# Gate and up products of a SwiGLU in seven half-size products instead of eight, with the weight differences formed by accumulating DMAs

## The chip, the cores and the metric

The kernel runs on one core of one Trainium2 chip. The metric is the device time of one execution in microseconds, lower is better. TensorE (PE) multiplies, with PEld the loading of its stationary operand; VectorE (DVE), ScalarE (ACT) and GpSimd (POOL) do the elementwise work; SyncE (SP) issues the plain DMAs.

## The reference

One layer of a transformer trunk in float32, for 512 tokens (plus 16 meta tokens in the attention) of width 1024:

```python
for i in range(DEPTH):            # DEPTH = 1
    mix = dsa_attention(h, w_in, w_o, rel_bias, k_top)
    h = layer_norm(ALPHA * h + mix, ln1_g, ln1_b)
    ffn = (jax.nn.silu(h @ w_gate) * (h @ w_up)) @ w_down   # 1024 -> 2816 -> 1024
    h = layer_norm(ALPHA * h + ffn, ln2_g, ln2_b)
return h[:, N_META:]
```

The change is in the two products `h @ w_gate` and `h @ w_up`, and in what prepares their operands and takes up their results.

## The kernel before

A float32 product is made of three products of a rounded type (float32r): each operand x is parted into hi (x rounded, a copy by ACT) and lo (x - hi, a subtraction, line 159), and hi\*hi, hi\*lo and lo\*hi are added up in PSUM (lines 286 to 288 for gate and up, line 1072 for the down product).

The order of the instructions on each engine is the order in which the Python code issues them (`manual_schedule`); a tile pool gives each tile a buffer, and a wait is put in where a buffer or a value is not yet free.

The stages of the program are the projections and the sparse attention (to about 300 us), the second half of the output projection with the first normalisation (to 313 us), gate and up (313 to 555 us), down (555 to 677 us) and the last normalisation.

Gate and up: the 2816 columns of each weight make 22 blocks f of 128 columns. For each block the chunks `wg{f}` and `wu{f}` (128 partitions x 8 K-tiles x 128 columns, 512 KB each) are loaded by SP two chunks ahead, parted one chunk ahead (`cut`, called by `ahead`; hi by ACT, lo of gate by DVE and lo of up by POOL), and multiplied with the 512 normalised tokens `h1h`, `h1l`, which lie turned (K on the partitions): 8 K-tiles x 3 terms x 2 weights make 48 matmuls of 128x512. Block 0 runs in two halves of 256 tokens, because the norms of the last two token blocks of 128 come late: `turn_norm` (line 971) turns token block b by TensorE and parts it. After each block ACT takes the silu of gate (line 1013), DVE multiplies it with up (line 1014), and the result is parted at once into `hh`, `hl`, which are the stationary operands of the down product.

Down: for each half `th` of the tokens, all 22 chunks of `wd` are loaded, parted and multiplied (line 1072).

Of the kernel before, what the change touches and what calls it, by code (L numbers as in the profile page):

```python
# [117 lines left out]
def trunk(ctx, tc, a, out):  # L118
# [848 lines left out]
    def turn_norm(b):  # L967
        for q in range(2):
            pt = bank(f"tz{b}{q}", "pt")
            for i in range(4):  # L970
# [4 lines left out]
            sub(nc.vector, lo, ptv, hi)

    for b in range(NB):
# [8 lines left out]
        if b == 0:  # L986
            load(g_ff, 2)


    hh, hl = [], []  # L990
    hq = []

    def widen(nm, o, n0, n1):
        wh, wl = chunk(nm)
        return mm3(
            o[:, n0:n1],
            ((wh[:, k * P : (k + 1) * P], wl[:, k * P : (k + 1) * P], h1h[k][:, n0:n1], h1l[k][:, n0:n1]) for k in range(KT)),
        )

    for f in range(NF):  # L1000
        pg = [bank(f"p_wg{f}", "mm"), bank(f"p_wu{f}", "S")]

        for n0, n1 in ((0, 2 * P), (2 * P, S)) if f == 0 else ((0, S),):
            for o, nm in zip(pg, (f"wg{f}", f"wu{f}")):
                if n1 == S:
                    ahead(nm)
                for k, _ in enumerate(widen(nm, o, n0, n1)):
                    if n1 < S and k == LATER_K:
                        turn_norm(2 + (nm == "wu0"))
        if f == NF - 1:  # L1010
            ahead("wd0_0")
        sg = third(f"sg{f}")[:, :S]
        nc.scalar.activation(sg, pg[0], AF.Silu)
        nc.vector.tensor_tensor(out=sg, in0=pg[1], in1=sg, op=ALU.mult)  # L1014
        if f < 8:
            if f % 4 == 0:
                hq.append((quad(f"hh{f}", S), quad(f"hl{f}", S)))
            hi, lo = (x[:, f % 4] for x in hq[f // 4])
        else:
            hi, lo = unit(f"hh{f}", F32R)[:, :S], unit(f"hl{f}", F32R)[:, :S]  # L1020
        act_copy(hi, sg)
        sub(nc.vector, lo, sg, hi)
        hh.append(hi)
        hl.append(lo)
# [129 lines left out]
```

## Time and profile before

| what | value |
|---|---|
| time, median of 3 runs | 685.97 us (685.8 to 687.2) |
| the profiled execution: its own time | 686.96 us |
| its span in the trace | 685.2 us |
| granted TensorE clock, mean | 0.996 of 2.4 GHz |
| PE busy | 669.6 us (98%) |
| DVE, ACT, POOL busy | 418.9, 287.3, 237.8 us |
| gate and up, blocks 1 to 21 | 326.7 to 555.2 us |

The page gives the busy time of each engine over the whole span. The views by line, by window and in order of time cut it into stages; the span and the time of the execution differ by 1.8 us that lie outside the trace.

### The profile page before, as it was taken

What the parts mean: (1) busy time and instruction counts of PE and PEld (TensorE: products, weight loads), DVE (VectorE), ACT (ScalarE), POOL (GpSimd) and SP (SyncE); (2) the same over time, 40 slices, a digit from 0 to 9 for tenths busy, and PEclk for the clock granted to TensorE, in tenths of its full rate; (3) what the DMA queues carried; (4) which work ended last, traced back from release to release, by engine and by line L of the source; (5) the groups of instructions that cost most, each with busy time, mean ns of one, the idle gap of its engine ahead of it and who ended that gap; (6) DMA issues with size and microseconds to landing.
All of it is one profiled execution on the core that took longest, in us unless ns stands there. A gap on an engine that the chain in (4) does not pass through costs nothing.

```text
span 685.2 us, 9428 instructions
## 1 busy us (share of the span) xinstructions
PE 669.6 (98%) x3440; PEld 565.6 (83%) x3440; DVE 418.9 (61%) x797; ACT 287.3 (42%) x516; POOL 237.8 (35%) x240
## 2 busy tenths in 40 slices
PE   8999999999999999999999999999999999999995
PEld 6888787889998888889888888888888888888884
DVE  5589897888888887696334243343433355575426
ACT  5473512567777775614323233232322334423310
POOL 2063812497786676653212121221212200011003
PEclk9999999999999999999999999999999999999998
DMA  6547130543133346410131322313132267745611
GB/s 235 173 148 258 58 75 17 152 152 85 56 103 87 93 114 211 154 62 31 63 122 63 123 80 105 114 70 123 61 123 83 102 224 233 244 152 193 195 51 61
DMA packets 31807, 83.11 MB, mean 121 GB/s; under 512 B 3745, under 2 KB 8913, under 8 KB 31761
## 3 DMA queue, kind: packets, MB, share of 16 engines
q1 hardware_dynamic: 31328, 82.12, 36.9%
q8 instruction: 27, 0.44, 0.3%
q10 hardware_dynamic: 432, 0.39, 0.2%
...
HBM read 74.86 MB, written 5.27 MB: 117 GB/s over the span
## 4 chain that ended last, share of the span: by engine, by line
PE 51%; DVE 1%; POOL 0%; DVEq 0%; issue 0%
PE pd L1072 17%; PE p_wu L288 6%; PE p_wu L287 6%; PE p_wu L286 6%; PE p_wg L288 6%; PE p_wg L287 6%; PE p_wg L286 6%; DVE su L1082 0%; POOL fr L939 0%; DVE y L1081 0%; DVE y L956 0%; PE tz L971 0%; DVE mw L1087 0%; DVEq L1150 0%; DVE y L958 0%
## 5 line engine op out<-in xcount | busy, mean ns | idle before, releaser
L159 POOL TENSOR_TENSOR l_wu<-r_wu,h_wu 128x1024 fp32r<-128x1024 f32 x22 | 52.8, 2401 | 179.5 <-ACT h_wu L156 179.5
L1014 DVE TENSOR_TENSOR sg<-p_wu,sg 128x512 f32<-128x512 f32 x22 | 15.2, 692 | 107.8 <-PE p_wu L288 107.8
L159 DVE TENSOR_TENSOR l_wd<-r_wd,h_wd 128x1024 fp32r<-128x1024 f32 x36 | 45.4, 1263 | 41.9 <-ACT h_wd L156 41.7
L286 PE MATMUL p_wg<-h1h,h_wg 128*128 128x512 f32 (+1 forms) x184 | 70.0, 380 | 0.0
L286 PE MATMUL p_wu<-h1h,h_wu 128*128 128x512 f32 (+1 forms) x184 | 70.0, 380 | 0.0
L287 PE MATMUL p_wg<-h1l,h_wg 128*128 128x512 f32 (+1 forms) x184 | 69.9, 380 | 0.0
L288 PE MATMUL p_wu<-h1h,l_wu 128*128 128x512 f32 (+1 forms) x184 | 69.9, 380 | 0.0
L287 PE MATMUL p_wu<-h1l,h_wu 128*128 128x512 f32 (+1 forms) x184 | 69.9, 380 | 0.0
L288 PE MATMUL p_wg<-h1h,l_wg 128*128 128x512 f32 (+1 forms) x184 | 69.9, 380 | 0.0
L159 DVE TENSOR_TENSOR l_wg<-r_wg,h_wg 128x1024 fp32r<-128x1024 f32 x21 | 52.8, 2513 | 24.4 <-ACT h_wg L156 24.4
L156 ACT ACTIVATE hh<-sg 128x512 fp32r<-128x512 f32 x22 | 13.9, 632 | 119.3 <-DVE sg L1014 119.3
L670 POOL TENSOR_TENSOR lg<-lg,rec 128x144 f32<-128x144 f32 (+1 forms) x64 | 52.6, 846 | 21.9 <-DVE rec L668 21.1
L1072 PE MATMUL pd<-h_wd,hh 128*128 128x512 f32 (+1 forms) x162 | 59.6, 368 | 0.0
L1072 PE MATMUL pd<-h_wd,hl 128*128 128x512 f32 (+1 forms) x162 | 59.6, 368 | 0.0
L1072 PE MATMUL pd<-l_wd,hh 128*128 128x512 f32 (+1 forms) x162 | 59.5, 368 | 0.0
L156 ACT ACTIVATE h_wd<-r_wd 128x1024 fp32r<-128x1024 f32 x36 | 38.0, 1060 | 46.5 <-DMA r_wd<-in_wd 22.2
L644 POOL TENSOR_TENSOR bm<-score,tz 128x256 f32<-128x256 f32 (+1 forms) x64 | 43.9, 716 | 16.4 <-DVE mn L653 14.9
L939 POOL TENSOR_TENSOR fr<-fr,half_neg 128x1 f32<-128x1 f32 x4 | 4.0, 1004 | 117.5 <-DVE fr L938 117.0
L661 ACT ACTIVATE lg<-lg,mn 128x272 f32<-128x272 f32 (+1 forms) x64 | 36.3, 571 | 11.6 <-DVE mn L653 11.6
L287 PEld LDWEIGHTS p_wu<-h1l,h_wu 128*128 128x128 f32 x184 | 34.6, 188 | 6.6
L286 PEld LDWEIGHTS p_wg<-h1h,h_wg 128*128 128x128 f32 x184 | 34.6, 188 | 6.5
L286 PE MATMUL p_k<-hTh,h_wk 128*128 128x264 f32 x128 | 37.7, 295 | 2.3 <-DVE q L329 2.3
...
## 6 DMA issues: line engine op xcount, KB each, us to landing
r_wd<-in_wd SPq DMA_DIRECT2D x36, 512.0 KB, 4.3
r_wg<-in_wg SPq DMA_DIRECT2D x22, 512.0 KB, 3.7
r_wu<-in_wu SPq DMA_DIRECT2D x22, 512.0 KB, 4.5
...
r_wq<-in_wq SPq DMA_DIRECT2D x8, 512.0 KB, 4.8
r_wk<-in_wk SPq DMA_DIRECT2D x8, 512.0 KB, 3.4
rbig<-rdram SPq DMA_DIRECT2D x1, 3072.0 KB, 15.0
...
```

The lines of the kernel that those rows point to most:

```text
L156: nc.scalar.activation(o, i, AF.Copy, scale=scale)
L159: eng.tensor_tensor(out=o, in0=x, in1=y.bitcast(F32), op=ALU.subtract)
L286: nc.tensor.matmul(o, lh, rh, start=i == 0, stop=False)
L287: nc.tensor.matmul(o, lh, rl, start=False, stop=False)
L288: nc.tensor.matmul(o, ll, rh, start=False, stop=i == KT - 1)
L644: nc.gpsimd.tensor_tensor(out=bm.at(b, W[b] - n, W[b]), in0=mask.at(b, W[b] - n, W[b]), in1=tzs[h][:, 256 - n :], op=ALU.add)
L661: nc.scalar.activation(lg.blk(b), lg.blk(b), AF.Exp, bias=mn[:, i : i + 1], scale=-1.0, accum_out=den[:, b : b + 1])
L670: nc.gpsimd.tensor_tensor(out=lg.blk(b), in0=lg.blk(b), in1=rec[:, b : b + 1].to_broadcast([P, W[b]]), op=ALU.mult)
L939: nc.gpsimd.tensor_tensor(out=r, in0=r, in1=half_neg, op=ALU.pow)
L1014: nc.vector.tensor_tensor(out=sg, in0=pg[1], in1=sg, op=ALU.mult)
L1072: nc.tensor.matmul(pd[o], l[:, bs], r[:, c0:c1], start=f == 0 and i == 0, stop=f == NF - 1 and i == 2)
```

## The change

A Strassen product (in Winograd's form) takes the place of the plain one in blocks 1 to 21. Three things are cut in two: the 1024 rows of K, the tokens (256 and 256), and the 256 columns of a block (its 128 of gate and its 128 of up). A plain 2x2 block product needs eight products of a quarter of the token matrix with a quarter of the weight block; this form needs seven, numbered 1 to 7 in the code, each of 4 K-tiles x 3 terms = 12 matmuls of 128x256, and sums of quarters before and after.

- **Token side.** The four quarters and four sums of them (`left_sum`: S1, S2 and two differences, by DVE and POOL) are parted once and kept in eight tiles `s{i}`.
- **Weight side.** The weights lie anew in DRAM: `wgu[f]` holds gate's upper half of K, up's upper half, up's lower half, gate's lower half, 512 columns each. SP loads the first two as `x` and the other two as `y`. The products 1, 2 and 3 take a quarter as it is. The products 5, 7, 6 and 4 take differences: ACT writes -x into the tile T (`sums_a`), and an accumulating DMA, issued by POOL (`plus`), adds the neighbouring 1024 columns from DRAM onto it in SBUF, which gives 5 and 7; `sums_b` then copies -(5) and adds 512 columns for 6, and `sums_c` copies -(6) and adds 512 columns for 4. The tile T has two buffers, so `sums_a` of block f+2 writes where block f's 5, 7 and 6 lay.
- **Parting.** `right_part` parts the 512 columns of each of the seven factors, hi by ACT and lo by DVE, `LEAD` - 1 = 3 products ahead. POOL parts no weights of this stage any more.
- **After a product.** `after` adds the products up: two share a PSUM bank where the form adds them, the others are added by DVE (five additions of 128x256 in a block), with two silus of 128x256 and a copy of 128x256 by ACT; product 7 goes into the bank out of which the addition `m` after product 6 has read, and product 3 into that of product 5.
- **The order** is written out in the list `order`: 8 products of block 0 (plain, in halves of tokens) with product 1 of block 1 among them, then for each block 5, 6, 2, 7, (1 of the next block), 4, 3. `due` puts the loads and sums at fixed distances ahead of a block's product 5 (20, 14, 10, 9 and 4 products).
- **Down.** The hidden values stay unparted (`hid`) and are parted at half width in the down stage, four chunks ahead (`hidden_parts`): 44 times 128x256 by ACT and DVE.
- `sums_a(1)` stands twice: once beside the second norm, once in `due` at the first product.

The orders below are those of the built programs; a number behind a name is a buffer's. First ACT, in a block of the middle of gate and up, before: two copies of 128x1024, one copy of 128x512 and one silu a block.

```order
L1013 ACTIVATE sg_4073<-p_wg_4011 128x512 [waits PE_49]
L156 ACTIVATE hh_3875<-sg_4073 128x512 [waits DVE_49]
L156 ACTIVATE h_wu_4080<-r_wu_4017 128x1024 [waits DMAHW6_49,Activation_49]
L156 ACTIVATE h_wg_4110<-r_wg_4047 128x1024 [waits DMAHW7_49,PE_49,Pool_49]
L1013 ACTIVATE sg_4073<-p_wg_4078 128x512 [waits PE_49]
```

ACT at the same place now (a line with T as both sides is `sums_b`, which waits for an accumulating DMA, DMASW; the line of 128x1024 is `sums_a` of the block after next; w_5, w_2 and so on are the hi parts of those factors).

```order
L159 ACTIVATE w_6_5279<-T_5051 128x512
L159 ACTIVATE T_5185<-T_5185 128x512 [waits DMASW1_49]
L159 ACTIVATE m_5297<-pa_5262 128x256 [waits PE_49]
L159 ACTIVATE w_2_5299<-ry 128x512 [waits DMAHW5_49]
L1170 ACTIVATE sg_5256<-sg_5256 128x256 [waits DVE_49]
L159 ACTIVATE w_7_5316<-T_5051 128x512 [waits Activation_49]
L159 ACTIVATE T_5319<-r_x_5207 128x1024 [waits DMAHW6_49,DVE_49]
L159 ACTIVATE w_1_5338<-r_x_5073 128x512 [waits PE_49]
L159 ACTIVATE w_4_5356<-T_5241 128x512 [waits DMASW2_49,PE_49]
L159 ACTIVATE w_3_5372<-ry 128x512 [waits PE_49]
L159 ACTIVATE T_5375<-T_5185 128x512 [waits DMASW3_49]
L1161 ACTIVATE sg_5390<-pa_5262 128x256 [waits PE_49]
```

ACT now waits three times a block for an accumulating DMA, and a copy that waits holds up all that stands behind it, the hi parts of the next factors among it. Next DVE before, one block:

```order
L1014 TENSOR_TENSOR sg_4073<-p_wu_4012,sg_4073 128x512 [waits PE_49,Activation_49]
L159 TENSOR_TENSOR hl_3876<-sg_4073,hh_3875 128x512 [waits Activation_49]
L159 TENSOR_TENSOR l_wg_4111<-r_wg_4047,h_wg_4110 128x1024 [waits DMAHW7_49,Activation_49]
L1014 TENSOR_TENSOR sg_4073<-p_wu_4079,sg_4073 128x512 [waits PE_49,Activation_49]
L159 TENSOR_TENSOR hl_4143<-sg_4073,hh_4142 128x512 [waits Activation_49]
```

and DVE now, one block (L162 is the lo part of a factor, L1147 an addition after a product, L1174 the multiplication of gate and up):

```order
L162 TENSOR_TENSOR w_2_5433<-ry,w_2_5433 128x512 [waits DMAHW7_49,Activation_49]
L1147 TENSOR_TENSOR sg_5390<-pe_5418,v_5409 128x256 [waits PE_49]
L162 TENSOR_TENSOR w_7_5450<-T_5185,w_7_5450 128x512 [waits Activation_49]
L1147 TENSOR_TENSOR uu_5410<-pd_5322,m_5297 128x256 [waits PE_49]
L1174 TENSOR_TENSOR hid_5470<-sg_5390,uu_5410 128x512 [waits DVE_49]
L162 TENSOR_TENSOR w_1_5472<-r_x_5207,w_1_5472 128x512 [waits DMAHW6_49,Activation_49]
L162 TENSOR_TENSOR w_4_5490<-T_5375,w_4_5490 128x512 [waits DMASW5_49,Activation_49]
L1147 TENSOR_TENSOR m_5431<-pb_5477,m_5431 128x256 [waits PE_49]
```

The additions, which free a PSUM bank for PE, now stand behind lo parts that wait for ACT. On PE, product 7 (last row) waits for DVE's addition m, one product after product 6:

```order
L1122 MATMUL pb_5879<-s_3914,w_6_5815 128x256 [waits DVE_49]
L1122 MATMUL pb_5879<-s_3914,w_6_5815 128x256 x9
L1122 MATMUL pa_5798<-s_3665,w_2_5835 128x256 [waits Activation_49]
L1122 MATMUL pa_5798<-s_3665,w_2_5835 128x256
L1122 MATMUL pa_5798<-s_3665,w_2_5835 128x256 [waits DVE_49]
L1122 MATMUL pa_5798<-s_3665,w_2_5835 128x256 x9
L1122 MATMUL pb_5879<-s_3936,w_7_5852 128x256 [waits DVE_49,Activation_49]
```

where before the first matmuls of a block waited only for the parts of its weights:

```order
L286 MATMUL p_wg_4011<-h1h_3559,h_wg_3977 128x512 [waits Activation_49]
L287 MATMUL p_wg_4011<-h1l_3560,h_wg_3977 128x512
L288 MATMUL p_wg_4011<-h1h_3559,l_wg_3978 128x512 [waits DVE_49]
...
L286 MATMUL p_wu_4012<-h1h_3559,h_wu_4013 128x512 [waits PE_49,Activation_49]
...
L288 MATMUL p_wu_4012<-h1h_3559,l_wu_4014 128x512 [waits Pool_49]
```

The last row's wait for POOL is gone, and each product's bank is now freed by an addition or a copy. The code of the change, cut to its core:

```diff
+LEAD = 4
+LOAD_X, SUM_A, LOAD_Y, SUM_B, SUM_C = 20, 14, 10, 9, 4
...
+    def left_sum(i):
+        if i == 5:
+            sums[1] = [unit(f"S1{j}")[:, :512] for j in range(2)]
+            combine(nc.vector, sums[1], quarter[1, 0], quarter[1, 1], ALU.add)
+            left_part(5, sums[1])
+        elif i == 6:
+            sums[2] = [unit(f"S2{j}")[:, :512] for j in range(2)]
+            combine(nc.gpsimd, sums[2], sums[1], quarter[0, 0], ALU.subtract)
+            combine(nc.gpsimd, quarter[1, 0], quarter[0, 0], quarter[1, 0], ALU.subtract)
+            left_part(6, sums[2])
...
+    order = whole[:4] + [(1, 1)] + whole[4:]
+    order += [(1, 2), (1, 5), (1, 6), (2, 1), (1, 7), (1, 4), (1, 3)]
+    for f in range(2, NF):
+        order += [(f, i) for i in (5, 6, 2, 7)] + [(f + 1, 1)] * (f + 1 < NF) + [(f, 4), (f, 3)]
+    base = [order.index((f, 5)) if f else 0 for f in range(NF)]
...
+    def plus(o, f, c0, c1):
+        nc.gpsimd.dma_start(o, a["wgu"][f][:, c0:c1], accum_op=ALU.add)
+
+    def sums_a(f):
+        t = wide(f"T{f}")
+        act_copy(t[:, :1024], upper[f], scale=-1.0)
+        plus(t[:, :1024], f, 512, 1536)
+        tsum[f, 5], tsum[f, 7], tsum[f, 6] = t[:, :512], t[:, 512:1024], t[:, 1024:1536]
+
+    def sums_b(f):
+        act_copy(tsum[f, 6], tsum[f, 5], scale=-1.0)
+        plus(tsum[f, 6], f, 1024, 1536)
+
+    def sums_c(f):
+        tsum[f, 4] = unit(f"T4{f}", tag="kq")[:, :512]
+        act_copy(tsum[f, 4], tsum[f, 6], scale=-1.0)
+        plus(tsum[f, 4], f, 1536, 2048)
...
+    def right_part(f, i):
...
+        hi, lo = right[f, i] = (t[:, :512], t[:, 512:])
+        act_copy(hi, x)
+        sub(nc.vector, lo, x, hi)
...
+    def terms(o, w, s, first, last):
+        (wh, wl), (sh, sl) = w, s
+        for k in range(4):
+            ks = slice(k * P, (k + 1) * P)
+            for j, (l, r) in enumerate(((wh, sh), (wh, sl), (wl, sh))):
+                nc.tensor.matmul(
+                    o, l[:, ks], r[:, k], start=first and k + j == 0, stop=last and k == 3 and j == 2,
+                    skip_group_check=not (first and last),
+                )
...
+        elif i == 6:
+            add(ev[f, "m"][:, hi], pf[f, "b"], ev[f, "m"][:, lo])
+        elif i == 7:
+            ev[f, "v"], ev[f, "u"] = unit(f"v{f}", tag="kq"), unit(f"uu{f}")
+            add(ev[f, "v"][:, lo], pf[f, "b"], ev[f, "m"][:, lo])
+            add(ev[f, "u"][:, hi], pf[f, "d"], ev[f, "v"][:, lo])
+        elif i == 4:
+            add(ev[f, "g"][:, hi], pf[f, "e"], ev[f, "v"][:, lo])
+            nc.scalar.activation(ev[f, "g"][:, hi], ev[f, "g"][:, hi], AF.Silu)
...
-    for f in range(NF):
-        pg = [bank(f"p_wg{f}", "mm"), bank(f"p_wu{f}", "S")]
...
+    for n, x in enumerate(order):
...
+        prepare(min(n + LEAD, len(order)))
+        due(n)
...
+        product(*x)
+        if n:
+            after(*order[n - 1])
...
+            if o == outs[0]:
+                hidden_parts(th * NF + f + 4)
```

## Rows read from the trace of the kernel before

**Rows 1.** The page, part 1 (busy, share, instructions) and TensorE's clock in 40 slices.
```profile
PE 669.6 (98%) x3440; PEld 565.6 (83%) x3440; DVE 418.9 (61%) x797; ACT 287.3 (42%) x516; POOL 237.8 (35%) x240
...
PEclk9999999999999999999999999999999999999998
```
**Rows 2.** Busy time by windows (us): gate and up's blocks 1 to 21, then down.
```profile
core 0: us, PE busy (x) PEld busy (x) DVE busy (x) ACT busy (x) POOL busy (x), PEclk, DMA share, GB/s
326.70:555.60 228.90, 228.90 (x1012) 189.61 (x1011) 84.53 (x65) 66.71 (x85) 50.41 (x21) 1.00 0.28 98
555.60:676.60 121.00, 121.00 (x589) 101.39 (x588) 63.96 (x73) 42.75 (x42) 6.96 (x8) 1.00 0.53 173
```
**Rows 3.** PE in order of time (start, length in us): 128x256, then 128x512, then down.
```profile
320.96 0.28 PE L286 MATMUL p_wg<-h1h,h_wg 128*128 128x256 f32 x1
321.08 0.28 PE L287 MATMUL p_wg<-h1l,h_wg 128*128 128x256 f32 x1
...
326.72 0.40 PE L286 MATMUL p_wg<-h1h,h_wg 128*128 128x512 f32 x1
...
555.22 0.39 PE L1072 MATMUL pd<-h_wd,hh 128*128 128x512 f32 x1
```
**Rows 4.** ACT in order of time, one block of gate and up.
```profile
382.14 0.63 ACT L156 ACTIVATE hh<-sg 128x512 fp32r<-128x512 f32 x1 [5.64 <-DVE sg L1014]
382.68 1.05 ACT L156 ACTIVATE h_wu<-r_wu 128x1024 fp32r<-128x1024 f32 x1
383.63 1.04 ACT L156 ACTIVATE h_wg<-r_wg 128x1024 fp32r<-128x1024 f32 x1
```
**Rows 5.** DVE in order of time: behind ACT's hh, two in a row, one of 128x256.
```profile
382.80 0.69 DVE L159 TENSOR_TENSOR hl<-sg,hh 128x512 fp32r<-128x512 f32 x1 [0.70 <-ACT hh L156]
...
305.57 1.29 DVE L159 TENSOR_TENSOR h1l<-tz,h1h 128x512 fp32r<-128x512 f32 x2 [0.48 <-ACT h1h L156]
...
202.37 0.42 DVE L159 TENSOR_TENSOR pt<-pt,pt 128x256 fp32r<-128x256 f32 x1
202.71 0.68 DVE L711 TENSOR_TENSOR bd<-pt,diag 128x512 fp32r<-128x512 f32 x1
```
**Rows 6.** Groups by line and shape (xcount, busy us, mean ns, idle before): ACT, DVE, POOL.
```profile
L156 ACT ACTIVATE pt<-pt 128x256 fp32r<-128x256 f32 x16 | 6.1, 380 | 0.6 <-PE pt L698 0.3
L1013 ACT ACT_TABLE_LOAD x1 | 1.3, 1283 | 2.5 <-PE p_wg L288 2.5
L159 DVE TENSOR_TENSOR l_wg<-r_wg,h_wg 128x1024 fp32r<-128x1024 f32 x21 | 52.8, 2513 | 24.4 <-ACT h_wg L156 24.4
L159 DVE TENSOR_TENSOR l_wd<-r_wd,h_wd 128x1024 fp32r<-128x1024 f32 x36 | 45.4, 1263 | 41.9 <-ACT h_wd L156 41.7
L159 POOL TENSOR_TENSOR wol<-r_wr,woh 128x512 fp32r<-128x512 f32 x4 | 5.1, 1297 | 2.6 <-ACT woh L156 2.6
L939 POOL TENSOR_TENSOR nr<-nr,half_neg 128x1 f32<-128x1 f32 x4 | 4.0, 993 | 8.3 <-DVE nr L938 8.3
```
**Rows 7.** SP's queue, two loads (start, length), and DMA issues: KB, median us to landing.
```profile
387.32 0.33 SPq L188 DMA_DIRECT2D r_wg<-in_wg  x1
387.74 1.07 SPq L188 DMA_DIRECT2D r_wu<-in_wu  x1
...
r_wg<-in_wg SPq DMA_DIRECT2D x2, 512.0 KB, 3.7
r_wu<-in_wu SPq DMA_DIRECT2D x2, 512.0 KB, 4.8
...
r_wo<-in_wo SPq DMA_DIRECT2D x4, 512.0 KB, 3.4
```
**Rows 8.** PE's longest wait of the whole span (total, times, longest).
```profile
PE p_k L286 <- DVE q L329: 2.3, 2, 1.3
```

More of the change, by code (lines that the diff above doesn't have):

```diff
@@ L975, in turn_norm, with left_part, combine @@
             sub(nc.vector, lo, ptv, hi)
+            for i in range(2):
+                act_copy(halves_of(quarter[half, q][i])[:, :, at], ptv[:, 2 * i : 2 * i + 2])
+    def left_part(i, x):
+        left[i] = left_quad(i)
+        hi, lo = (z.rearrange("p (j i) n -> p j i n", i=2) for z in left[i])
+        for j in range(2):
+            act_copy(hi[:, j], halves_of(x[j]))
+            sub(nc.vector, lo[:, j], halves_of(x[j]), hi[:, j])
+    def combine(eng, o, x, y, op):
+        for j in range(2):
+            eng.tensor_tensor(out=o[j], in0=x[j], in1=y[j], op=op)
@@ new lines, in due @@
+    def due(n):
+        for f in range(2, NF):
+            for back, what in ((LOAD_X, load_x), (LOAD_Y, load_y)):
+                if n == base[f] - back or n == 0 and base[f] - back < 0:
+                    what(f)
+        for f in range(1, NF):
+            for back, what in ((SUM_A, sums_a), (SUM_B, sums_b), (SUM_C, sums_c)):
+                at = max(base[f] - back, order.index((f - 2, 7)) - LEAD + 1 if f > 2 and back == SUM_A else 0)
+                if n == at:
+                    what(f)
@@ new lines, in trunk, with prepare, hidden_parts @@
+    prepared = [0]
+    def prepare(n):
+        for x in order[prepared[0] : n]:
+            right_part(*x[:2])
+        prepared[0] = max(prepared[0], n)
+    parts2, pq4 = {}, []
+    def hidden_parts(n):
+        while len(parts2) < min(n, 2 * NF):
+            i = len(parts2)
+            if i % 4 == 0:
+                pq4.append(quad(f"hp{i}", 512))
+            x = pq4[-1][:, i % 4]
+            z = hid[i % NF][:, i // NF * HT : i // NF * HT + HT]
+            parts2[i // NF, i % NF] = (x[:, :HT], x[:, HT:])
+            parted(x[:, :HT], x[:, HT:], z, nc.vector)
@@ L986, in trunk @@
         if b == 0:
[L987 to L998, printed above, removed]
-    for f in range(NF):
-        pg = [bank(f"p_wg{f}", "mm"), bank(f"p_wu{f}", "S")]
[L1003 to L1024, printed above, removed]
+            prepare(2)
+        if b == 1:
+            prepare(4)
+            load_y(1)
+            sums_a(1)
+    for n, x in enumerate(order):
+        if n == 1:
+            turn_norm(2)
+        if n == 4:
+            turn_norm(3)
+        prepare(min(n + LEAD, len(order)))
+        due(n)
+        if n == 5:
+            left_sum(5)
+        if n == 6:
+            left_sum(6)
+        if n == 7:
+            left_sum(7)
+        if n == 9:
+            left_sum(3)
+        product(*x)
+        if n:
+            after(*order[n - 1])
+        if n == len(order) - 8:
+            load(g_ff, 0)
+            load(g_ff, 1)
+        if n == len(order) - 4:
+            hidden_parts(4)
+        if n == len(order) - 2:
+            cut(g_ff, 0)
+    after(*order[-1])
     gb2 = {}
```

107 lines of the change are left out of this document (93 added, 14 removed).

## The prediction

> **What bounds the kernel now.** Look first at the page: PE is busy for 98% of the span, at full granted clock until the tail [rows 1]. By windows, PE has no gap in blocks 1 to 21 of gate and up (228.9 of 228.9 us) nor in down, while DVE, ACT and POOL are busy for 84.5, 66.7 and 50.4 us of the same 228.9 [rows 2]. PE's longest wait in the whole span sums to 2.3 us and lies in an early stage [rows 8]. So gate and up is bound by the number and length of its matmuls. In order of time one matmul of 128x512 starts 0.2267 us after another: 1008 of them run from 326.72 to 555.22 us, 10.88 us a block [rows 3]. The 128x256 form is in the trace too: 48 of them run from 320.96 to 326.72 us, 0.1200 us each [rows 3]. That is 6% more per column, and it is all that the smaller matmul costs, so the change can be priced from rows.
>
> **Matmuls.** A block of seven products has 84 matmuls of 128x256: 84 x 0.1200 = 10.08 us, or 1.44 us a product. Against 10.88 that saves 0.80 us a block, 21 x 0.80 = 16.8 us. Block 0 keeps its 96 matmuls of 128x256. This is the most that the change can give; all else takes from it, because the work of the other engines now has to fit into 10.08 us.
>
> **Work of ACT and DVE.** In a row on ACT, a copy of 128x512 takes 0.54 us until the next starts (0.63 us to its own end) and one of 128x1024 0.95 (1.05) [rows 4]; one of 128x256 is 0.38 long, so about 0.30 apart [rows 6]. A block now has seven hi parts, `sums_a`, `sums_b`, `sums_c` and three ops of 128x256: 7 x 0.54 + 0.95 + 2 x 0.54 + 3 x 0.30 = 6.7 us (3.2 before, 66.7 over 21 [rows 2]). On DVE a lo part of 128x512 takes 0.60 in a row (1.29 for two, 0.69 for one) and an op of 128x256 0.34 (202.37 to 202.71; 0.42 long) [rows 5]: 7 x 0.60 + 5 x 0.34 + 0.60 for the final multiplication = 6.5 us. Both sums are below 10.08, so neither engine is the bound by its work. POOL loses its parting of the weights, which paid nothing here.
>
> **The loop through the accumulating DMA.** What counts is who waits for whom. The tile T has two buffers, so one loop runs through every block. `sums_a` of block f+1 ends; its accumulating DMA lands L later; then ACT takes in order `sums_b` (0.54), the copy m (0.30) and w_2 (0.63 to its end), DVE the lo of w_2 (0.60) and behind it the addition after product 4 (0.42), ACT the silu that needs it (0.30) and w_7 (0.63), DVE the lo of w_7 (0.69), and only then may ACT write `sums_a` of block f+2 (1.05), since that overwrites the buffer which the lo of w_7 reads. Engine to engine, a start follows the end it waits for by 0.03 us (382.77 to 382.80) [rows 4, 5]; five such steps make 0.17. Sum: 0.54 + 0.30 + 0.63 + 0.60 + 0.42 + 0.30 + 0.63 + 0.69 + 1.05 + 0.17 = 5.33 us. One round of the loop is one block, so a block takes the longer of 10.08 and L + 5.33, and L is hidden up to 4.75 us. Three factors are prepared ahead, which helps against a single late part, but not against a loop that comes round each block. PE meets the loss at product 7, which waits for the addition m, which stands on DVE behind the lo of w_4, which waits for ACT.
>
> **The price of L.** No DMA here accumulates, none is issued by POOL, so L has bounds. Below: a plain load of 512 KB by itself lands 3.4 us after its issue [rows 7]. Above: two loads of 512 KB issued 0.42 us apart land 3.7 and 4.8 us after their own issues, so 1 MB takes 0.42 + 4.8 = 5.2 us from the first issue [rows 7]; an issue by POOL may cost what its shortest instruction takes, 0.99 instead of SP's 0.33 [rows 6, 7], +0.7; and x and y of later blocks, 512 KB each, are issued as buffers come free at that same time, +1.1 (the distance of 3.7 to 4.8) if one is ahead: 7.0. I take 5.2: an accumulation of 512 KB must fetch 512 KB from DRAM and as much of what it adds to, so the nearest row is that of 1 MB. Then a block takes 10.53 us, and over the 19 blocks in which the loop has closed (3 to 21) it costs 19 x 0.45 = 8.6 us. Each further microsecond of L costs 19 us. `sums_b` and `sums_c` move half the bytes and have 5 and 6 products (7.2 and 8.6 us) until they are needed; they stay hidden.
>
> The Trainium skill, "Collectives: The Full Stack", section "The bandwidth ceiling: the fold count and why AG ≠ RS ≠ AR", says that such an add is slow because it needs two source reads, not because adding costs cycles; no run here shows it. By that the 1 MB row is the right one.
>
> **The start.** Block 1 has no lead. Its sums of tokens need the last norm, and they are queued: after the last quarter copies ACT and DVE do S1 (2 x 0.60) and its parts (2 x 0.54), then m, w_2 and `sums_c` (1.4); POOL issues that DMA (about 1.0) before S2 (2 x 1.30 [rows 6]); ACT waits with the parts of S2, then takes w_5, `sums_b` of block 2, two parts of the next sum (together 2.7), the table load (1.28 [rows 6]), a silu (0.54) and w_6 with its lo (1.3). That is 13.1 us until product 6 of block 1, in which PE has some five and a half products (7.9 us) to run: it waits about 5 us in products 5 and 6. Behind w_6 come w_1, two parts of S3, w_7, `sums_a` of block 3, a silu, w_4, its lo and m, about 6.5 us against two products (2.9): 4 more. The second `sums_a(1)` adds 0.95 of ACT. I take 10 us lost, bounds 5 (POOL's sums run beside the parts) and 13. The table load was there before too, but behind PE's work.
>
> **Down.** 44 partings of 128x256 add 13.2 us to ACT (0.30 each) and 15.0 to DVE, which have 42.8 and 64.0 of 121 us [rows 2]: hidden by the matmuls; if not, about 0.7 us each. The first `wd` chunk is parted two products ahead: nothing, at most 1 us. The end after the last matmul is as it was.
>
> **The sum.** The profiled execution took 686.96 us, 1.76 beyond its span and 0.99 above the median of three. 686.96 - 16.8 + 8.6 + 10 = 688.8 us, that is 1.8 us more than before; set on the median, 687.8 us. From no change a measurement of this kernel can tell about 0.2%, 1.4 us.
>
> **Rivals.**
> 1. The DMA lands within 4.75 us, the loop never closes, and only the start costs: 686.96 - 16.8 + 10 = 680.2 (675 to 683). For it: the lone load of 3.4 us, and that both reads might run side by side; ACT and DVE have a third of each block free. Against it: 1 MB in 5.2, and the loads in the same stretch. The Trainium skill, "DMA: Bandwidth & Descriptors", section "Anatomy of one DMA — SWDGE (gpsimd) path", fits a DMA issued by GpSimd at 2.0 us plus its bytes at 436 GB/s; for 512 KB that is 3.2 us, which would be this case; it is for a plain copy, and no row here shows one from that queue.
> 2. The accumulating DMAs queue with the plain loads in the loop. A block now moves 1 MB of plain loads and adds 1 MB, twice the bytes from DRAM, with a DMA share of 0.28 before [rows 2]. With L = 6.5 a block takes 11.83 us: 680.2 + 19 x 1.75 = 713.5, slower. The sum passes no change at L = 5.1 and 1.4 us more than that at 5.2, so this side begins where my forecast stands.
> 3. The lo parts stretch. With POOL at work beside it, DVE's l_wg of 128x1024 took 2.51 us against 1.26 for l_wd without [rows 6]. If POOL's issuing did the same, two lo parts in the loop would take 0.6 more each, L + 6.5: 688.8 + 19 x 1.2 = 712. Against it: POOL has no elementwise work left in the steady blocks.
>
> **How the numbers follow.** Forecast (L between 4.9 and 6.0), 0.45: 687.8 on the median, its own range 682 to 703; of this 0.08 is faster by over 0.2% (L below 5.0), 0.09 within 0.2%, 0.28 slower. On the median too, rival 1, 0.30: 679; rival 2, 0.17: 712; rival 3, 0.08: 711. So faster 0.30 + 0.08 = 0.38, same 0.09, slower 0.28 + 0.17 + 0.08 = 0.53. The range 676 to 710 leaves out the best starts of rival 1 (0.08) and the longer half of rivals 2 and 3 (0.12). The forecast is the likeliest mechanism, not a sure sign: a change of 0.4 us in L crosses no change.
>
> **What would show it.** In the trace after: matmuls of 128x256 0.120 us apart within a product (if 0.114, 10 us more are gained); PE's waits in blocks 3 to 21 at one place, the first matmul of product 7, on DVE's m, about 0.45 us each; ACT's idle time before the `sums_b` copy put down to the DMA into T, and that DMA 5.2 us from POOL's issue to its landing; about 10 us of PE's waits in block 1, at products 5, 6 and 7. If ACT's copies never wait for T, rival 1 holds; if the DMA share goes to 0.8 and L beyond 6, rival 2; if lo parts of 128x512 take over 1 us, rival 3. The forecast is wrong also if PE waits at other products than 7, for then another loop than mine is the bound.

## The result, and the profile after

The changed kernel takes 712.49 us (median of 4 runs, 711.31 to 714.63) beside 685.88 for the kernel before on the same chip: a ratio of 1.039, 95% interval 1.0356 to 1.0423. It is 26.6 us slower; forecast were 1.8 us slower, with a range of 676 to 710. The profiled execution took 713.49 us, its span is 711.7.

The page of the kernel after: engines, the chain that ended last by engine, the accumulating DMAs (count, KB, median us to landing).

```profile
PE 664.7 (93%) x4196; PEld 594.5 (84%) x4196; DVE 514.0 (72%) x1066; ACT 388.8 (55%) x775; POOL 243.4 (34%) x285
...
PE 30%; issue 26%; DMA 17%; DVE 12%; ACT 11%; POOL 4%; SPq 0%; DVEq 0%; POOLq 0%; ACTq 0%
...
T<-in_wgu POOLq DMA_DIRECT2D x22, 512.0 KB, 5.4
T<-in_wgu POOLq DMA_DIRECT2D x42, 256.0 KB, 6.3
```

PE's share falls from 98% [rows 1] to 93%, and a DMA now stands in the chain with 17%. Down begins at 581.49 us instead of 555.22 [rows 3], 26.27 later, so all of the loss lies in gate and up and just ahead of it. The first matmul of down, then PE's waits from 300 to 600 us (total, times, longest), and three windows of gate and up:

```profile
581.49 0.40 PE L1288 MATMUL pd<-h_wd,hp 128*128 128x512 f32 x1
...
PE pb L1122 <- DVE m L1147: 17.3, 19, 4.5
PE tz L1005 <- ACT q L159: 6.2, 5, 2.4
PE pd L1122 <- DVE w L162: 2.5, 1, 2.5
PE pd L1122 <- ACT w L159: 1.9, 1, 1.9
...
330.00:340.00 10.00, 8.20 (x47) 7.61 (x48) 4.54 (x7) 6.41 (x13) 1.71 (x2) 0.66 0.83 196
...
400.00:450.00 50.00, 46.55 (x381) 45.69 (x380) 32.78 (x60) 31.07 (x60) 12.08 (x14) 1.00 0.83 188
450.00:500.00 50.00, 47.47 (x390) 46.77 (x389) 31.65 (x58) 31.60 (x61) 12.00 (x14) 1.00 0.84 193
```

Where PE had no gap before [rows 2], it now waits in nearly every block, at the first matmul of product 7 (pb, 19 times for DVE's m), as the prediction said. Product 7 of block 2 starts at 369.06 us and that of block 21 at 577.2 (three products ahead of down): 208.1 us for 19 blocks, **10.95 a block** where its matmuls take 10.08. That is 16.6 us lost in the loop. The rest is the start: product 7 of block 2 is the 20th product, so without a wait it would stand, by estimate, at 313.15 (the first gate/up matmul before) + 19 x 1.44 + 1.7 for the 16 transposes between = 342.2 us. It is **26.9 us late**. And -16.8 + 16.6 + 26.9 = 26.7, which is the 26.27 of the stage within 0.5.

**The loop.** One block in order of time, rows of ACT, POOL's issue and lo parts on DVE:

```profile
442.84 1.06 ACT L159 ACTIVATE T<-r_x 128x1024 f32<-128x1024 f32 x1 [0.76 <-DVE w L162]
444.19 0.86 POOL L1064 DMA_DIRECT2D T<-in_wgu  x1 [3.78 <-ACT T L159]
...
449.71 0.63 ACT L159 ACTIVATE T<-T 128x512 f32<-128x512 f32 x1 [2.00 <-DMA T<-in_wgu]
450.51 0.62 ACT L159 ACTIVATE w<-ry 128x512 fp32r<-128x512 f32 x1
451.17 0.69 DVE L162 TENSOR_TENSOR w<-ry,w 128x512 fp32r<-128x512 f32 x1 [1.75 <-ACT w L159]
452.23 0.42 ACT L1170 ACTIVATE sg<-sg 128x256 f32<-128x256 f32 x1 [1.09 <-DVE sg L1147]
452.55 0.62 ACT L159 ACTIVATE w<-T 128x512 fp32r<-128x512 f32 x1
453.20 0.69 DVE L162 TENSOR_TENSOR w<-T,w 128x512 fp32r<-128x512 f32 x1 [1.01 <-ACT w L159]
453.92 1.06 ACT L159 ACTIVATE T<-r_x 128x1024 f32<-128x1024 f32 x1 [0.76 <-DVE w L162]
```

`sums_a` ends at 443.90; POOL issues its DMA 0.29 later; ACT's `sums_b` (T<-T) can start at 449.71: L = 5.81. From there w_2 and its lo, the silu of `sg`, w_7 and its lo lead to the next `sums_a`, which ends at 454.98: 5.27. This round is 11.08 us; the mean of 10.95 a block means an L of about 5.7.

**The start.** PE in order of time, first the row of the kernel before with its first gate/up matmul, then the kernel after. tz are the transposes of the norms, pg and pu the plain products of block 0, pd and pb products 5 and 7 of block 1, at the end product 7 of block 2:

```profile
313.15 0.28 PE L286 MATMUL p_wg<-h1h,h_wg 128*128 128x256 f32 x1
```

```profile
311.89 0.66 PE L1005 MATMUL tz<-ident,y 128*128 128x128 f32 x4 [2.40 <-ACT q L159]
313.80 1.11 PE L1005 MATMUL tz<-ident,y 128*128 128x128 f32 x4 [1.25 <-ACT q L159]
...
318.38 1.60 PE L1122 MATMUL pg<-s,w 128*128 128x256 f32 x12
...
328.61 0.66 PE L1005 MATMUL tz<-ident,y 128*128 128x128 f32 x4 [1.25 <-ACT q L159]
...
333.62 4.99 PE L1122 MATMUL pg<-s,w 128*128 128x256 f32 x24 [1.65 <-ACT s L159]
...
344.85 0.50 PE L1122 MATMUL pd<-s,w 128*128 128x256 f32 x2 [1.93 <-ACT w L159]
347.88 2.50 PE L1122 MATMUL pd<-s,w 128*128 128x256 f32 x10 [2.52 <-DVE w L162]
...
358.02 2.90 PE L1122 MATMUL pb<-s,w 128*128 128x256 f32 x12 [4.53 <-DVE m L1147]
...
369.06 1.66 PE L1122 MATMUL pb<-s,w 128*128 128x256 f32 x12 [0.84 <-DVE m L1147]
```

The first gate/up matmul starts at 318.38 instead of 313.15. Block 0 then loses 4.5 us to waits (tz, pa and pg), block 1 and product 7 of block 2 lose 9.8. Behind several of these waits matmuls run for a while at the lower level, 1.2 of 2.4 GHz (granted clock 0.66 from 330 to 340 us, 0.50 from 348 to 350 and from 358 to 360): the 24 of pg take 4.83 us for 2.88, the 12 of pb 2.70 for 1.44, the 10 of pd 2.30 for 1.20; 4.3 us together. With the 5.2 us by which the first matmul is late, that is 23.8 of the 26.9; the rest lies in smaller pieces.

### The profile page after: what moved, and what is told of

Same layout as the page of the kernel before. It is cut to its first block, busy times and chain, and to the rows that moved or that the text cites. A ratio compares the mean times of both kernels' runs of the same rounds, so it can differ in the third digit from the quotient of the medians.

```text
span 711.7 us, 11623 instructions
## 1 busy us (share of the span) xinstructions
PE 664.7 (93%) x4196; PEld 594.5 (84%) x4196; DVE 514.0 (72%) x1066; ACT 388.8 (55%) x775; POOL 243.4 (34%) x285
## 3 DMA queue, kind: packets, MB, share of 16 engines
HBM read 97.40 MB, written 5.27 MB: 144 GB/s over the span
## 4 chain that ended last, share of the span: by engine, by line
PE 30%; issue 26%; DMA 17%; DVE 12%; ACT 11%; POOL 4%; SPq 0%; DVEq 0%; POOLq 0%; ACTq 0%
DMA T<-in_wgu 15%; ACT T L159 4%; DVE w L162 4%; ACT w L159 3%; PE av L728 3%; PE pv L290 2%; PE pv L288 2%; PE pv L289 2%; PE pt L698 2%; PE p_q L290 2%; PE p_q L289 2%; PE p_q L288 2%; PE p_k L288 1%; PE p_k L290 1%; PE p_k L289 1%
## 5 line engine op out<-in xcount | busy, mean ns | idle before, releaser
L1288 PE MATMUL pd<-h_wd,hp 128*128 128x512 f32 (+1 forms) x324 | 91.1, 366 | 0.0
L1122 PE MATMUL pb<-s,w 128*128 128x256 f32 x504 | 70.2, 290 | 17.9 <-DVE m L1147 17.3
L1122 PEld LDWEIGHTS pb<-s,w 128*128 128x128 f32 x504 | 64.6, 195 | 21.3 <-ACT T L159 11.6
L162 DVE TENSOR_TENSOR w<-T,w 128x512 fp32r<-128x512 f32 x84 | 57.8, 688 | 28.3 <-ACT w L159 26.9
L1122 PE MATMUL pd<-s,w 128*128 128x256 f32 x504 | 65.5, 286 | 4.4 <-DVE w L162 2.5
L1122 PE MATMUL pa<-s,w 128*128 128x256 f32 x504 | 68.3, 285 | 0.2 <-DVE w L162 0.2
L1122 PEld LDWEIGHTS pd<-s,w 128*128 128x128 f32 x504 | 63.1, 195 | 4.9 <-DVE w L162 2.7
L1288 PEld LDWEIGHTS pd<-h_wd,hp 128*128 128x128 f32 x324 | 58.6, 189 | 10.1
L162 DVE TENSOR_TENSOR l_wd<-r_wd,h_wd 128x1024 fp32r<-128x1024 f32 x36 | 44.0, 1225 | 29.0 <-ACT h_wd L159 28.6
L1122 PEld LDWEIGHTS pa<-s,w 128*128 128x128 f32 x504 | 64.1, 194 | 0.5 <-DVE w L162 0.4
L1288 PE MATMUL pd<-l_wd,hp 128*128 128x512 f32 (+1 forms) x162 | 59.8, 369 | 0.7 <-DVE l_wd L162 0.7
L162 DVE TENSOR_TENSOR w<-ry,w 128x512 fp32r<-128x512 f32 x40 | 27.5, 688 | 31.6 <-ACT w L159 31.6
```

The lines of the kernel that those rows point to most:

```text
L162: eng.tensor_tensor(out=o, in0=x, in1=y.bitcast(F32), op=ALU.subtract)
L1122: nc.tensor.matmul(o, l[:, ks], r[:, k], start=first and k + j == 0, stop=last and k == 3 and j == 2, skip_group_check=not (first and last),)
L1288: nc.tensor.matmul(pd[o], l[:, bs], r[:, c0:c1], start=f == 0 and i == 0, stop=f == NF - 1 and i == 2)
```

## The experiments

Each ran beside the kernel before on its own chip. "Product 7" is its start in block 2, "a block" the mean distance from there to product 7 of block 21, which stands 4.32 us (three products) ahead of the first matmul of down.

| kernel | time, us | ratio (95%) | product 7 | a block |
|---|---|---|---|---|
| after | 712.49 | 1.039 (1.0356 to 1.0423) | 369.1 | 10.95 |
| e1_third_buffer | 694.23 | 1.0119 (1.0081 to 1.0156) | 366.6 | 10.20 |
| e2_plain_dma | 695.71 | one run | 365.0 | 10.21 |
| e3_no_loads | 713.82 | one run | 367.8 | 10.98 |
| e4_dve | 712.77 | 1.0383 (1.0366 to 1.0401) | 362.8 | 11.30 |
| e11_dve_behind | 733.61 | 1.07 (1.0656 to 1.0744) | 363.6 | 12.25 |
| e14_dve_order | 688.74 | 1.0037 (1.0022 to 1.0053) | 361.1 | 10.08 |
| e5_banks | 709.38 | 1.0341 (1.0313 to 1.0369) | 366.9 | 10.88 |
| e6_s2_dve | 707.91 | 1.032 (1.0291 to 1.0348) | 365.7 | 10.90 |
| e7_plain1 | 702.3 | 1.0238 (1.021 to 1.0266) | 359.6 | 10.86 |
| e9_first_pool | 709.76 | 1.0352 (1.0308 to 1.0395) | 368.7 | 10.90 |
| e12_early | 708.88 | 1.0318 (1.0293 to 1.0343) | 365.1 | 10.99 |
| e8_all | 681.83 | 0.9926 (0.9898 to 0.9954) | 354.2 | 10.13 |
| e10_all_pool | 684.06 | 0.9973 (0.9956 to 0.9989) | 355.3 | 10.18 |
| e13_all_early | 680.7 | 0.9896 (0.9868 to 0.9923) | 350.1 | 10.24 |
| e15_dve_all | 676.52 | 0.9867 (0.985 to 0.9883) | 349.0 | 10.08 |

**e1_third_buffer: is it the loop?**

```diff
-UNITS = {"u": 28, "kq": 14}
+UNITS = {"u": 26, "kq": 14}
...
-        t = wide(f"T{f}")
+        t = wide(f"T{f}") if f % 3 else up.tile([P, 1024], F32, name=f"T{f}", tag="T", bufs=1)
...
-        tsum[f, 5], tsum[f, 7], tsum[f, 6] = t[:, :512], t[:, 512:1024], t[:, 1024:1536]
+        tsum[f, 5], tsum[f, 7], tsum[f, 6] = t[:, :512], t[:, 512:1024], unit(f"T6{f}", tag="kq")[:, :512]
```

> A third buffer for the tile T (T6 goes to a small tile of its own, two small tiles fewer elsewhere for room); all work stays. Theory A, the loop: a block takes L + 5.27 us because sums_a of block f+2 must wait for the lo of w_7 of block f, which waits by way of sums_b for the accumulating DMA. With a third buffer one round of the loop spans two blocks, 11.08 us of 2 x 10.08, so ACT's waits for DVE ahead of sums_a go (15.1 us over 19), product 7's start-to-start distance falls from 11.08 to 10.1-10.3, and the time to 712.5 - 19 x 0.85 = about 696 (694 to 699). Theory B, the DMA engines: they are busy 0.83-0.85 of each steady stretch, and by the queue rows 1.05 MB of accumulation takes 6.1 us of all sixteen and 1.05 MB of loads 3.2, 9.3 of a block's 11.08. If they are the bound, an earlier sums_a only waits longer in the queue: L grows, the distance stays at 10.8 or more, 709 to 713.

Measured 694.23 us, 18.3 less, and a steady stretch without a gap (window, then the accumulating DMAs):

```profile
400.00:450.00 50.00, 50.00 (x419) 50.00 (x418) 34.41 (x66) 34.43 (x65) 12.95 (x15) 1.00 0.91 210
...
T<-in_wgu POOLq DMA_DIRECT2D x14, 512.0 KB, 5.3
```

Theory A holds. The DMA is as long as before, and the DMA engines are busier (0.91 instead of 0.83), yet PE stands nowhere in this stretch: the missing buffer closed the loop, not the DMA engines. The 10.20 a block of the table is no loop either: 1.6 us are matmuls at the lower clock right behind product 7 of block 2, 0.7 one wait at the end.

**e2_plain_dma and e3_no_loads: what makes L long?**

```diff
-        nc.gpsimd.dma_start(o, a["wgu"][f][:, c0:c1], accum_op=ALU.add)
+        nc.gpsimd.dma_start(o, a["wgu"][f][:, c0:c1])
```

> The same DMAs from POOL with the same bytes and places, but they copy instead of adding, so the differences of weights are left out of the computation. Theory A1 (the addition is what makes L long, since it reads from two places): L falls from 5.8 to 4.4 or less, near a plain load of 512 KB (3.4 alone, 4.8 behind another), the loop is hidden, product 7's distance is 10.1, about 696 us. Theory A2 (the issue by POOL, 0.86 us, and the x and y loads beside it make L long, not the addition): L stays at 5.4 or more, distance above 10.7, 706 to 712 us.

```diff
+        if f > 4:
+            upper[f] = upper[f - 3]
+            return
         upper[f] = raw(f"r_x{f}")[:, :1024]
...
             lower[f] = lower[2 + f % 2]
+            if f > 3:
+                return
```

> From block 4 or 5 on no x and y is loaded (the weights of earlier blocks are used again, so later blocks get a mix of weights); the accumulating DMAs stay. Theory A2 or B (loads and additions share the DMA engines): L falls to 4.8 or below, distance 10.1, DMA share from 0.84 to about 0.55, about 698 us. Theory A1 (the addition alone): L stays within 0.3 of 5.8 and the distance above 10.7, 707 to 712 us.

POOL's queue (packets, MB, share of the 16 engines) and its 512 KB DMAs from 400 to 560 us, first of the kernel after:

```profile
q0 software_dynamic: 6221, 15.25, 55.7%
...
T<-in_wgu POOLq DMA_DIRECT2D x15, 512.0 KB, 5.4
```

Then of e2_plain_dma, and of e3_no_loads:

```profile
q0 software_dynamic: 4427, 15.24, 29.2%
...
T<-in_wgu POOLq DMA_DIRECT2D x14, 512.0 KB, 3.6
```

```profile
q0 software_dynamic: 6319, 15.44, 55.7%
...
T<-in_wgu POOLq DMA_DIRECT2D x14, 512.0 KB, 5.3
```

Copying instead of adding lands 512 KB in 3.6 us, holds the engines for half as long, and opens the loop (695.71 us). Without the x and y loads the adding DMA still takes 5.3 and the time is 713.82, as long as with them. So the addition is the price (A1), not the loads beside it: A2 and rival 2's reason fall.

**e4_dve, e11_dve_behind, e14_dve_order: the same differences by DVE.**

```diff
-        act_copy(t[:, :1024], upper[f], scale=-1.0)
-        plus(t[:, :1024], f, 512, 1536)
...
+        less(nc.vector, tsum[f, 5], upper[f][:, 512:], upper[f][:, :512])
...
```

> The four differences of a block are made by DVE from the loaded weights (4 x 0.60 us), with no accumulating DMA and no copies by -x on ACT; for block 1 all stand beside the start. Theory A: no loop; DVE 6.5 + 2.4 = 8.9 and ACT 4.7 of 10.08 us a block, distance 10.1-10.3, worth 19 x 0.85 = 16; in the start ACT no longer stands behind a DMA (sums_b of blocks 1 and 2), worth 4 to 8 of the 26 lost there: 688 to 693. Rival C: DVE is busy 88% and takes its work in order, so its additions come late for product 7 and PE waits there as before: distance 10.7 or more, 700 or more.

No DMA was left to wait for, and nothing was won: 11.30 us a block. DVE and PE in order of time around product 7, whose row starts at 453.61:

```profile
450.03 0.69 DVE L1175 TENSOR_TENSOR hid<-sg,uu 128x512 f32<-128x512 f32 x1
450.64 0.69 DVE L162 TENSOR_TENSOR w<-r_x,w 128x512 fp32r<-128x512 f32 x1
450.96 1.60 PE L1123 MATMUL pa<-s,w 128*128 128x256 f32 x12
451.24 0.69 DVE L1064 TENSOR_TENSOR T<-r_x 128x512 f32<-128x512 f32 x1
451.84 0.69 DVE L162 TENSOR_TENSOR w<-T,w 128x512 fp32r<-128x512 f32 x1
452.45 0.69 DVE L1064 TENSOR_TENSOR T<-ry,T 128x512 f32<-128x512 f32 x1
...
453.05 0.42 DVE L1148 TENSOR_TENSOR m<-pb,m 128x256 f32<-128x256 f32 x1
...
453.61 0.36 PE L1123 MATMUL pb<-s,w 128*128 128x256 f32 x1 [1.05 <-ACT w L159]
```

Product 6 is over when product 2 (pa) starts at 450.96, but its addition m stands on DVE behind five ops that run back to back, and product 7 follows m by 0.14 us. (The row names ACT's copy of a later factor, which ends at nearly the same time and which product 7 does not read.) So rival C came true, and two reasons are possible: DVE is too full, or its order is wrong. e11 put the differences behind the additions (its edit against e4):

```diff
-LOAD_X, SUM_A, LOAD_Y, SUM_B, SUM_D, SUM_C = 20, 6, 10, 5, 3, 1
+LOAD_X, SUM_A, LOAD_Y, SUM_B, SUM_D, SUM_C = 20, 4, 10, 3, 1, 0
...
             after(*order[n - 1])
+        due(n, (sums_a, sums_b, sums_d, sums_c))
```

> e4_dve with the same four differences on DVE, but each queued behind the additions of the products instead of ahead of them (the difference for factor 5 and 6 two and two products later, those for 7 and 4 two and one). Theory C1 (in e4 DVE is not full, 8.9 of 10.08 us, but product 7 waits for the addition m, which stands in DVE's queue behind two lo parts and two differences): distance falls from 11.36 to 10.1-10.5 and the time from 712.8 to 693-700. Theory C2 (DVE is full): distance 10.9 or more, 705 to 713.

Worse, 733.61 us: both theories as written missed. ACT and DVE in order of time show why:

```profile
449.59 0.68 DVE L1064 TENSOR_TENSOR T<-r_x 128x512 f32<-128x512 f32 x1
...
450.37 0.63 ACT L159 ACTIVATE w<-T 128x512 fp32r<-128x512 f32 x1 [1.56 <-DVE T L1064]
...
451.03 0.69 DVE L162 TENSOR_TENSOR w<-T,w 128x512 fp32r<-128x512 f32 x1 [0.76 <-ACT w L159]
```

DVE comes to the lo straight after its own difference and idles 0.76 us for ACT's hi between them, at three of the four factors of a block, 0.18 at the fourth. PE's waits there also bring the lower clock: the granted clock is 0.93 from 400 to 450 us, so part of the 12.25 is slower matmuls. e14 only moves each difference one product ahead (its edit against e11):

```diff
-LOAD_X, SUM_A, LOAD_Y, SUM_B, SUM_D, SUM_C = 20, 4, 10, 3, 1, 0
+LOAD_X, SUM_A, LOAD_Y, SUM_B, SUM_D, SUM_C = 20, 5, 10, 4, 2, 1
```

> The differences on DVE once more, each queued behind the additions of the products and one product earlier than in e11, so that ACT's hi of a factor is done when DVE comes to its lo. Theory C1' (in e11 DVE stood idle 0.76 us at each of four differences because the lo came right behind its difference, and ACT's hi lies between; its work of 8.9 us would fit): distance 10.1-10.5, 693 to 700 us. Theory C2 (with 8.9 us of work in order DVE meets product 7 late in any order): 10.9 or more, 705 or more.

```profile
400.00:450.00 50.00, 50.00 (x419) 50.00 (x418) 46.27 (x85) 25.34 (x50) 0.00 (x0) 1.00 0.32 106
```

10.08 us a block with DVE busy 93% of the time, and 688.74 us, better than expected: C1' holds, C2 falls. The same work in three orders costs 10.08, 11.30 and 12.25 us a block.

**The start: e5_banks, e6_s2_dve, e7_plain1, e9_first_pool, e12_early,** one edit each on the kernel after. The intervals of e5 and e9 overlap that of the kernel after, so their times alone show little. e5 copies the quarters from the bank first and makes the parts from them:

```diff
-            act_copy(hi, ptv)
-            sub(nc.vector, lo, ptv, hi)
+            z = [halves_of(quarter[half, q][i])[:, :, at] for i in range(2)]
             for i in range(2):
-                act_copy(halves_of(quarter[half, q][i])[:, :, at], ptv[:, 2 * i : 2 * i + 2])
+                act_copy(z[i], ptv[:, 2 * i : 2 * i + 2])
+            for i in range(2):
+                act_copy(hi[:, 2 * i : 2 * i + 2], z[i])
+                sub(nc.vector, lo[:, 2 * i : 2 * i + 2], z[i], hi[:, 2 * i : 2 * i + 2])
```

> Only the turning of the norms is changed: ACT first copies both halves of the PSUM bank to the quarters (2 x 0.30 us), and the hi and lo parts are made from the quarters, so the bank is free without DVE. Start theory D (PE stands at the transposes because a bank stays taken until ACT's quarter copies, which wait for DVE's lo of the same bank, 0.76 us each): PE's waits at tz (6.2 us) go to 1 or less, the matmuls at half clock about 314 to 316 us with them (about 1.5): 712.5 - 6 = about 706 (704 to 708). Rival E: the chain through the last norm, ACT, DVE and POOL in block 1 ends at the same time whatever PE does before, so what is won at tz is waited for in block 1: product 7 of block 2 stays at 368 to 369 us and the time at 711 to 713.

-3.1 us, between D and E: tz waits 1.2 us instead of 6.2, but 4.6 of these 5.0 us come back at pg, which now waits 6.3 instead of 1.7; product 7 of block 2 comes 2.2 us sooner.

```diff
-            combine(nc.gpsimd, sums[2], sums[1], quarter[0, 0], ALU.subtract)
-            combine(nc.gpsimd, quarter[1, 0], quarter[0, 0], quarter[1, 0], ALU.subtract)
+            combine(nc.vector, sums[2], sums[1], quarter[0, 0], ALU.subtract)
+            combine(nc.vector, quarter[1, 0], quarter[0, 0], quarter[1, 0], ALU.subtract)
```

> Only the two token sums of S2 and the two of the quarter difference move from POOL (2.85 and 2.79 us for two, behind an issue of 0.86) to DVE (4 x 0.60). Theory F (the start is set by ACT waiting in order for S2 with w_5 behind it): PE's waits at products 5 and 7 of block 1 (1.9 + 2.5 + 4.5) shrink by 3 to 5 us together: 707 to 710. Rival G: ACT and DVE are full there anyway (their own 13 us of work), and DVE now has 2.4 more: 712 to 714.

-4.6 us: F holds, the waits at product 5 are gone (product 7's grows to 5.2).

```diff
-    order = whole[:4] + [(1, 1)] + whole[4:]
-    order += [(1, 2), (1, 5), (1, 6), (2, 1), (1, 7), (1, 4), (1, 3)]
+    plain = lambda half, *qs: [(1, q, half) for q in qs]
+    order = whole[:4] + plain(0, "11", "21") + whole[4:] + plain(0, "12", "22")
+    order += plain(1, "11", "12") + [(2, 1)] + plain(1, "21", "22")
...
```

> Block 1 too is done by plain products (8 instead of 7, +1.44 us), so that block 2 is the first to need sums of tokens and of weights, with 8 products more of cover; the second sums_a(1) goes. Theory H (the 26 us lost in the start are the missing lead of block 1): the waits of block 1 (1.9 + 2.5 + 4.5 us and its matmuls at half clock, 2.4) and some of those at tz go, -10 to -14, +1.4: 700 to 704. Rival E': the chain of ACT and DVE is as long as the cover and only moves: 708 or more.

-10.2 us: H holds, with an eighth product in block 1.

```diff
-        sub(nc.vector, lo, x, hi)
+        sub(nc.gpsimd if n < 4 else nc.vector, lo, x, hi)
```

> Only the lo parts of block 0's four weights go back from DVE to POOL, where they were before the change. Theory I: on DVE they stand between the ops of norms 1 and 2 and stretch to 1.5 us beside POOL's own work, so norm 2 and the first gate/up matmul come late (318.4 against 313.2 us before); on POOL they free about 4 us of DVE: first matmul at 315 to 316.5, 709 to 711 us, since part of it is waited for again in block 1. Rival J: POOL's power and multiplications of the norms then stand behind the lo parts (about 1.3 us each) and nothing is won: 712 to 714.

-2.7 us, but the first gate/up matmul comes at 317.83, only 0.55 sooner. Theory I falls by this, though the time lies in its range: the engine alone is not the point. Rival J's reason is in the trace: DVE reaches the next norm at 302.38 us instead of 305.34, but POOL's power (nr) stands behind two lo parts and starts at 305.67, where it started at 305.51. e12 moves both parts, hi and lo, to where the kernel before made them, into the output projection ahead of the norms, with lo on POOL:

```diff
+            if k > 3:
+                for q in ("11", "21") if k == 4 else ("12", "22"):
+                    first_part(q)
...
```

> Only the hi and lo parts of block 0's four weights are made earlier: during products 4 and 5 of the output projection's last part but one, where before made them (lo on POOL), instead of behind norms 0 and 1. Theory K (these eight ops on ACT and DVE in the norms' way are the 5.2 us by which the first gate/up matmul is late, whichever engine makes the lo): first matmul at 314 to 316 us instead of 318.4, total 708 to 711, the rest being waited for again in block 1. Rival L (the transposes' wait for the bank and the quarters' copies alone make it late): 317.5 or later, 712 to 713.

```profile
313.45 0.38 PE L1137 MATMUL pg<-s,w 128*128 128x256 f32 x1 [0.19 <-ACT s L159]
```

The first gate/up matmul comes at 313.45 (before: 313.15), so theory K holds for that place; of the 4.9 us won there 3.6 stay in the total.

**All together: e8_all, e10_all_pool, e13_all_early, e15_dve_all.** e8 has the edits of e1, e5, e6 and e7 and moves the sums of block 2 (below); e10 adds that of e9 and has these sums at 2, 6 and 9; e13 is e8 with that of e12; e15 has those of e5, e6, e7, e12 and e14.

```diff
...
-                at = max(base[f] - back, order.index((f - 2, 7)) - LEAD + 1 if f > 3 and back == SUM_A else 0)
+                at = {SUM_A: 6, SUM_B: 10, SUM_C: 13}[back] if f == 2 else max(base[f] - back, order.index((f - 2, 7)) - LEAD + 1 if f > 3 and back == SUM_A else 0)
```

> The third buffer of e1 with the three edits of the start (banks, sums on DVE, block 1 plain), and the sums of block 2 a few products later. If loop and start are all of the loss and add up: e1's 694.2, less the 23.7 us that its product 7 of block 2 is late (366.6 against 342.9 us with no wait), of which 3 to 8 stay (norms 2 and 3 are themselves late), + 1.4: 673 to 680, that is faster than before (686.2) by 1 to 2%. If the start only moves, 685 to 692.

> e8_all with the same move of block 0's lo parts to POOL, and the sums of block 2 begun right behind norm 0's turning (products 2, 6 and 9 instead of 6, 10 and 13). By theory I the first gate/up matmul comes at 313 to 314 us instead of 316.1, without the matmuls at half clock behind it (about 3 us in e8_all), and the waits at product 1 and 7 of block 2 (0.9 + 0.6 + 2.1) shrink: 681.8 - 5 = 675 to 678. By rival J no better than e8_all, 680 to 684.

> e8_all with the same early parts. By theory K the first gate/up matmul comes at 313 to 314 us (316.1 in e8_all) with no half-clock matmuls behind it (12 took 3.0 us for 1.44): 681.8 - 4 = 676 to 679. By rival L 680 to 684.

> The differences by DVE in e14's order (no accumulating DMA) with the four edits of the start (quarters first from the bank, token sums on DVE, block 1 plain, block 0's parts early). If loop and start are two separate losses, both are gone here without a DMA: product 7 of block 2 at 348 to 352 us, then 10.08 us a block with DVE busy above 0.9, gate and up ending at 547 to 550 us, 676 to 680 us. If DVE at 0.9 cannot carry the start's sums as well, waits of 3 us or more appear in blocks 2 and 3 and the time is 682 to 686.

e8 is faster than before, by 0.7%, a little short of what was expected. e13 wins 4.1 us more at product 7 but 1.1 in all, which the two intervals cannot tell from nothing, and its blocks take 10.24 for 10.13. Of these 2.0 us, 1.5 are the clock: the wait at product 7 of block 2 is as long in e8, e13 and e15 (2.06, 2.05, 1.98 us), but only in e13 the 24 matmuls from there on run mostly at the lower level (granted clock 0.58 from 350 to 354 us) and take 4.43 us for 2.88. First e13, then e15:

```profile
350.09 2.42 PE L1140 MATMUL pb<-s,w 128*128 128x256 f32 x12 [2.05 <-DVE m L1165]
```

```profile
349.00 1.67 PE L1141 MATMUL pb<-s,w 128*128 128x256 f32 x12 [1.98 <-DVE m L1166]
```

e10 is 2.2 us worse than e8; it has two edits more, so the move to POOL is not priced by itself, but the trace shows what it costs. DVE's four lo parts of 128x256 in e8_all, then the same in e10_all_pool with POOL beside it:

```profile
309.93 1.42 DVE L162 TENSOR_TENSOR s<-q,s 128x256 fp32r<-128x256 f32 x4
```

```profile
308.23 3.61 DVE L162 TENSOR_TENSOR s<-q,s 128x256 fp32r<-128x256 f32 x4 [1.89 <-ACT s L159]
...
308.32 1.47 POOL L162 TENSOR_TENSOR w<-r_x,w 128x512 fp32r<-128x512 f32 x1
309.75 1.47 POOL L162 TENSOR_TENSOR w<-r_y,w 128x512 fp32r<-128x512 f32 x1
```

In e10 two of the four take about 1.5 us each, as long as POOL's ops beside them, where one took 0.41: what POOL takes over, DVE pays back. e15 is the fastest, 676.52 us, 1.3% faster than before: product 7 of block 2 at 349.0, then 10.08 us a block, and down begins at 544.90 (555.22 before). Loop and start are separate losses, and both can go. Against a start without waits e15 still loses 5.4 us (349.0 - 342.2 - 1.44); which of its waits are the last to go was not tried.

## Why the prediction was wrong

- **Matmuls: right.** The 12 of product 7 start 0.120 us apart; 10.08 us a block is what e14 and e15 reach.
- **Work of ACT and DVE: right as a bound.** Put at 6.7 and 6.5 us a block, they are 6.8 and 7.2 in the kernel after (31.1 and 32.8 of 50 us). Neither engine limits the kernel after. In e14 DVE carries 9.3 us a block (0.93 of 10.08) and PE has no gap.
- **The loop: mechanism and place right.** The part from the landing to the next `sums_a` was put at 5.33 and is 5.27; PE pays at product 7; e1 takes the loop away with a third buffer. The additions of 256 KB stay hidden as said, though they land 6.3 us after their issue.
- **The price of L: mis-sized, the first term that failed.** 5.2 was taken, about 5.7 is what the loop sees on the mean (5.81 in the block shown): 0.29 from the end of ACT's copy to POOL's issue, then 5.4 to the landing. The row of 1 MB of plain loads was near. But L was defined from the end of `sums_a` and priced from the issue on, so the 0.29 stood in no term. A block was put at 10.53 and takes 10.95 on the mean: 16.6 us for 8.6. The forecast itself called this the sore point, 19 us for each microsecond.
- **The start: the term that failed most,** 26.9 us for 10 (bounds 5 to 13). The waits named there, in block 1, were about right: 9.0 us at products 5 and 7. What was left out lies ahead of them. Block 0's parts were moved into the norms' stretch, and the sum put that at nothing (e12: 4.9 us at the first matmul). The quarter copies were counted as work of ACT, but they wait for DVE's lo of the same PSUM bank and hold the bank till then (tz waits 6.2 us; without that the time is 3.1 less, e5, at the edge of the noise). And no price was set on the lower clock behind some of the waits (4.3 us in rows). These pieces overlap. By the prediction's sum neither miss alone leaves the range (696.8 us with 16.6 for the loop, 705.7 with 26.9 for the start); both together make 713.7.
- **The rivals.** Rival 1 fell: L is above 4.75. Rival 2 gave nearly the measured time, 712, by luck: the DMA share did go to 0.84, but L is the same without the loads (e3), a block takes 10.95 and not 11.83, and the start makes up the difference. Rival 3 fell for the steady blocks, where a lo part of 128x512 takes 0.69; in the start it is real, 1.5 us beside POOL's norm work:

```profile
302.16 1.51 DVE L162 TENSOR_TENSOR w<-r_y,w 128x512 fp32r<-128x512 f32 x1
```

- **Down: right.** From its first matmul to the end of the span it takes 130.2 us, 130.0 before.
- **The sides.** That the loop, not DVE's or ACT's load, takes back the gain of the matmuls was right (-16.8 + 16.6); the loss is made by the start.
